# The second of two feature tiles in another order of products, and the inner operands of a Strassen-style FFN made later

## The chip, the cores and the metric

The kernel runs on one core of a Trainium2 chip. The time is the device time of one execution, in microseconds (us). The core has a matrix engine (TensorE, PE in the profile; its weight loads are listed apart as PEld), a vector engine (VectorE, DVE), a scalar engine (ScalarE, ACT), a general one (GpSimd, POOL) and a sequencer that issues DMAs (SyncE, SP). Each runs its own queue in order; they meet through semaphores. Matmuls write to accumulators in PSUM, and VectorE and ScalarE read them from there.

## The reference

One layer of a hybrid decoder for 1,048 tokens: 16 learned meta tokens and 1,024 prompt tokens as one sequence, and 8 single sample tokens with states of their own. The model width is 1,024 and the FFN width 2,816, all in float32:

```python
h = h + 0.5 * swiglu(rmsnorm(h, n1), w1g, w1u, w1d)     # first FFN
u = rmsnorm(h, nm) @ w_in                               # 4 HGRN2 heads and 8 Mamba-2 heads
...                                                     # scans, gates, norms
h = h + mix                                             # the output projection
h = h + 0.5 * swiglu(rmsnorm(h, n2), w2g, w2u, w2d)     # second FFN
y = rmsnorm(h, norm_final)
```

with `swiglu(x, wg, wu, wd) = (silu(x @ wg) * (x @ wu)) @ wd`. The change touches the gate and up half of both FFNs, `x @ wg` and `x @ wu`.

## The kernel before

**Precision.** Each float32 operand is split into a high part (a cast on ScalarE to the matmul's format) and a low part (the difference, on VectorE). A product is three matmuls, high by high, high by low, low by high (`mm3`, lines 163 to 165). Almost all matmuls of the kernel bear these three lines.

**Seven products for eight.** Gate and up projections of a feature tile of 128 columns are computed together. The weights form a 2 by 2 block matrix (gate or up, first or second half of the 1,024 rows) and the activations another (first or second half of the rows, first or second part of the tokens). Their product is made by a Winograd-Strassen scheme with seven block products, numbered 1 to 7, on sums of blocks. Tokens come in two halves c = 0, 1 of two quarters each (262 columns in the first FFN, 258 in the second). One *step* is one product on one half: four blocks of 128 rows by three matmuls, 12 matmuls. `Steps` is a list of such steps, written out by hand. `S.before(i, fn)` hangs other work ahead of step i, and `S.add(mm, post)` adds a step with what follows it. Within the two FFNs the order of PE, DVE, ACT and SP is this written order (`manual_schedule`, line 988). Outside of them a planner orders the engines other than PE by estimated times.

**Accumulators.** Products 2, 3 and 4 are added in PSUM onto 1, 5 and 7 (`Unit.bank`: `{2: 1, 3: 5, 4: 7}`); 1, 6, 5 and 7 need an accumulator of their own. `K.banks(2)` leaves two accumulators, each of two banks, one bank a token half. A new product must wait until the one that held the accumulator before has been read. Those reads are in `post` in `pair`: product 1 is copied out by ScalarE (z, line 674); product 6 is added to z (v, L676); product 2 is multiplied by the norm's factor (`times_r`, L669) and goes through SiLU (L681); product 5 is added to v (x, L683); product 7 to x (u1, L685); product 4 to v (L698), then scaled (L669) and multiplied by the gate (`product_`, L718).

**Pairs.** A loop of eleven passes, i = 0 to 10, takes two feature tiles each (`ffn`, line 993). In the passes 0 to 2 a tile has all seven products in the order 1, 6, 2, 5, 7, 3, 4, 14 steps. From i = 3 on, product 3 of the two tiles is not computed by itself: the two product-3 weight blocks and the product-3 activations form one more 2 by 2 problem, which `Inner` solves with seven smaller products. The first tile of such a pair runs 1, 6, 2, 5, 7; its product 4 comes behind the second tile's product 1 (`inner.last`). The second tile then goes on with 6, 2, 5, 7, between and behind which the inner products stand.

**Weights.** Four raw blocks a tile are loaded by SP ten or so steps ahead (`Left.load`, L452), summed on DVE (L458), cast on ACT (`hi`, L462) and given their low part on DVE (`lo`, L466). `left.plan` hangs these at steps relative to the tile's first; the last argument says at which step each product's weights are due, in the order given, and the cast is hung four steps ahead, the low part three. The inner weights have L597 and L601.

**Inner operands.** The activations of the inner problem are sums of pieces of block 3, so they are made once in an FFN. `Inner.operands` returns fourteen jobs (add back high and low part, L558; differences L571 to L574; casts L564; low parts L567) and two late ones, which `ffn` hangs at steps of the passes i = 1 and 2.

**Hidden.** The products of gate and up are stored to DRAM (`Hidden.jobs`, differences L818, stores L821 on SP) and come back for the down projection (`down`, operands split at L842 and L846, weights at L903 and L908). SP issues loads of weights and these stores in one queue.

Of the kernel before, what the change touches and what calls it, by code (L numbers as in the profile page):

```python
# [490 lines left out]
class Unit:  # L491
# [25 lines left out]
    def both(self, S):  # L517
        for p in ORDER:
            for c in range(2):
                self.step(S, p, c, (0, 1))  # L520


def halves(t):
    return t.rearrange("p (c t) -> p c t", c=2)


ORDER6 = (1, 6, 2, 5, 7, 4)


class Inner:  # L530
# [118 lines left out]
def pair(K, S, wg, wu, f, ops, spread, hid, late_r, first=None, inner=None):  # L649

    nc = K.nc
    fs = slice(f * P, f * P + P)
    s0 = len(S.steps)
    wait = late_r > 14
    tm = {}
    left = Left(K, [wg[:, 0:4, fs], wu[:, 0:4, fs], wu[:, 4:8, fs], wg[:, 4:8, fs]], 4)  # L660

    def temp(n, cs):
        if n not in tm:
            tm[n] = halves(K.t(2 * K.Q))
        return tm[n][:, cs]

    def times_r(n, i, cs, src=None):
        t = temp(n, cs)
        nc.vector.tensor_mul(t, t if src is None else src, spread.lanes(i, cs))  # L669
        return t  # L670

    def post(p, cs, b):
        if p == 1:
            nc.scalar.copy(temp("z", cs), b)
        elif p == 6:
            nc.vector.tensor_add(temp("v", cs), b, temp("z", cs))  # L676
        elif p == 2 and (f == 0 or wait and f == 1):
            nc.scalar.copy(temp("g0", cs), b)
        elif p == 2:
            t = times_r("g0", 0, cs, b)  # L680
            nc.scalar.activation(t, t, AF.Silu)  # L681
        elif p == 5:
            nc.vector.tensor_add(temp("x", cs), b, temp("v", cs))  # L683
        elif p == 7:
            nc.vector.tensor_add(temp("u1", cs), b, temp("x", cs))  # L685
            if inner:
                times_r("u1", 1, cs)
        elif p == 3:
            nc.vector.tensor_add(temp("g1", cs), b, temp("v", cs))
            if f == 0:  # L690
                return
            if wait and f == 1:
                silu(0, cs)
            silu(1, cs)
            times_r("u1", 1, cs)
        elif inner:
            t = temp("v", cs)
            nc.vector.tensor_add(t, b, t)  # L698
            tm["u0"] = tm["v"]
            times_r("u0", 0, cs)  # L700
            product_(0, cs)
        else:
            nc.vector.tensor_add(temp("u0", cs), b, temp("v", cs))
            if f == 0:
                return
            times_r("u0", 0, cs)
            for n in range(2):
                product_(n, cs)

    def silu(n, cs):  # L710
        t = times_r(f"g{n}", n, cs)
        nc.scalar.activation(t, t, AF.Silu)  # L712

    def product_(n, cs):
        if "h" not in tm:
            tm["h"] = True
            hid.append(K.slot("s", K.T))
        nc.vector.tensor_mul(halves(hid[0][:, n * 2 * K.Q : n * 2 * K.Q + 2 * K.Q])[:, cs], temp(f"g{n}", cs), temp(f"u{n}", cs))  # L718

    if inner:  # L720
        i = f % 2
        left.plan(S, s0, 0, 2 * i, ORDER6, ((0, 2, 4, 6, 8, 12), (0, 4, 6, 8, 10, 14))[i])
        unit = Unit(K, left.w, [o.op for o in ops], 4, post)

        def both(*ps):
            for p in ps:
                for c in range(2):
                    unit.step(S, p, c, (0, 1))

        def keep():  # L730
            inner.raw[i] = left.raw[3]

        cs = slice(0, 2)

        def gate():
            tm["g1"] = tm["x"]
            silu(1, cs)

        S.before(s0, keep)
        inner.then[i] = (gate, lambda: product_(1, cs))  # L740
        inner.out[i] = lambda: temp("x", cs)
        if i == 0:
            both(1, 6, 2, 5, 7)
            inner.last = lambda: both(4)
            return
        S.before(s0 + 3, lambda: inner.begin(S, s0 + 2))
        both(1)
        inner.last()
        both(6, 2, 5, 7)
        inner.step(S, 1, 6)  # L750
        inner.step(S, 5, 7)
        both(4)
        inner.step(S, 2, 3)
        inner.step(S, 4)
        e = len(S.steps)
        for at, fn in ((0, inner.then[0][0]), (2, inner.then[1][0]), (3, inner.then[0][1]), (5, inner.then[1][1])):
            S.before(e + at, fn)
        return

    if not first:  # L760
        left.plan(S, s0, int(f == 1), 3 * int(f == 1))
        Unit(K, left.w, [o.op for o in ops], 4, post).both(S)
        return

    late = {}

    def post_first(p, cs, b):

        if p == 5:
            late[p] = b  # L770
        else:
            post(p, cs, b)
            if p == 6:
                post(5, cs, late[5])

    order = first(S, left)
    unit = Unit(K, left.w, [o.op for o in ops], 4, post_first)
    for ps_ in (order[:6], order[6:]):
        for c in range(2):
            for p in ps_:  # L780
                unit.step(S, p, c, (c,), True)
    cs = slice(0, 2)
    for i, (fn, *args) in enumerate(((silu, 0, cs), (silu, 1, cs), (times_r, "u0", 0, cs), (product_, 0, cs), (times_r, "u1", 1, cs), (product_, 1, cs))):
        S.before(s0 + late_r + i, lambda fn=fn, args=args: fn(*args))
# [193 lines left out]
def ffn(K, wg, wu, wd, ops, spread, src, first, after, late_r):  # L978

    NF = DFF // P
    wgv = wg.rearrange("(k p) c -> p k c", p=P)
    wuv = wu.rearrange("(k p) c -> p k c", p=P)
    wdv = wd.rearrange("(f p) c -> p f c", p=P)
    E = mybir.EngineType

    with K.tc.manual_schedule(engines={E.PE, E.DVE, E.Activation, E.SP}):
        S = Steps()
        S.before(14, lambda: K.banks(2))  # L990
        hidden = Hidden(K)
        inner = Inner(K, ops)
        for i in range(NF // 2):
            hid, e = [], []
            rec = inner.next() if i >= 3 else None
            if i == 1:

                def operands(s0=len(S.steps) + 8):
                    made, late = inner.operands()
                    for n, fn in enumerate(made):  # L1000
                        S.before(s0 + 3 * n, fn)
                    for n, fn in enumerate(late):
                        S.before(s0 + 56 + 3 * n, fn)

                S.before(len(S.steps) + 7, operands)
            for f in (2 * i, 2 * i + 1):
                hid.append([])
                pair(K, S, wgv, wuv, f, ops, spread, hid[-1], late_r, first if f == 0 else None, rec)
                e.append(len(S.steps))
            hidden.jobs(S, i, hid, *([late_r + 6, max(late_r + 7, e[1])] if i == 0 else e), rec)  # L1010
        h = []
        down(K, S, wdv, hidden, src, h, after)
        S.run()
    return h
# [878 lines left out]
class LastFinal:  # L1893
# [11 lines left out]
    def first(self):  # L1905
        K = self.K
        self.st = K.sml.tile([P, 6, 3], F32, tag="ssl", name="ssl", bufs=1)
        self.yt = [K.slot("u", D) for i in self.tiles]
        for j, i in enumerate(self.tiles):
            ps = K.psm()  # L1910
            for k in range(4):
                self.transpose(ps, k, k, i)
            self.square(j, ps, 0, 4, 0)
            K.nc.vector.tensor_mul(self.yt[j][:, :512], ps, self.nf[0][:, :512])
# [27 lines left out]
def body(ctx, tc, a, o):  # L1942
# [86 lines left out]
    def after1(S, h, e3, e0, e1):  # L2029
# [33 lines left out]
        return nm.add  # L2063

    ffn(K, a["w_ffn1_gate"][0], a["w_ffn1_up"][0], a["w_ffn1_down"][0], ops, spread, from1, first1, after1, 26)

    constants_mix(K, a)
# [142 lines left out]
    def after3(S, h, e3, e0, e1):  # L2210
# [16 lines left out]
        return None  # L2227

    ffn(K, a["w_ffn2_gate"][0], a["w_ffn2_up"][0], a["w_ffn2_down"][0], ops2, spread2, lambda o: hd2[o], first2, after3, 14)


# [35 lines left out]
```

## Time and profile before

| | before |
|---|---|
| median of 3 runs | 1996.66 us (1996.43 to 2001.31) |
| the profiled execution | 1997.03 us, its span 1995.2 us |
| granted TensorE clock, mean | 0.992 |
| TensorE busy | 1931.3 us (97%), 16,585 matmuls |
| VectorE busy | 1532.8 us (77%) |
| ScalarE busy | 858.9 us (43%) |
| DMA | 258.45 MB, mean 130 GB/s |

The page of the profile tells for one execution how long each engine was busy, which chain of work ended last, and groups of instructions by line. Behind it stand answers of the trace: who waited for whom, busy time by stretch, and the instructions of an engine in order of time. In a timeline a row is start, length, engine, line, operation, output and inputs; in brackets is the idle time of the engine ahead of the row and what ended it. Matmuls overlap, so for TensorE the distance of two starts tells more than their lengths.

### The profile page before, as it was taken

The page shows a single profiled execution, that of the slowest core. Times are in us where ns is not written, and L with a number is a line of the kernel's source. Part 1 is how long each engine was busy: PE and PEld are TensorE (multiplying, and loading weights), DVE is VectorE, ACT ScalarE, POOL GpSimd, SP SyncE. Part 2 cuts the span into 40 slices and gives each one's busy share as a digit, 9 for nine tenths or more (in the row PEclk, how much of TensorE's full clock was granted, in tenths as well). Part 3 has the DMA queues.
Part 4 walks back from the last instruction along what each step waited for, and adds up shares of the span by engine and source line. Part 5 has one row for each costly group of instructions (what it writes and reads, how often), then busy time and mean ns, then how long its engine had stood idle before and what let it go on. Part 6 is the DMA issues. An engine that isn't in the chain of part 4 may idle for free.

```text
span 1995.2 us, 40967 instructions
## 1 busy us (share of the span) xinstructions
PE 1931.3 (97%) x16585; PEld 1889.7 (95%) x16585; DVE 1532.8 (77%) x2720; ACT 858.9 (43%) x1647; POOL 83.1 (4%) x135
## 2 busy tenths in 40 slices
PE   7999999999999999999999999999999999999997
PEld 6999999999999999998988989999999999999997
DVE  7787888888788876576755547888888888878974
ACT  7532233233533644465644535743222332354352
POOL 4000000000000410000000001200000000000000
PEclk9999999999999999999999999999999999999999
DMA  7223333335977542232532253224232333577851
GB/s 217 75 87 106 91 100 100 101 93 158 279 233 244 165 145 55 59 101 64 164 90 71 62 167 126 83 80 128 81 106 88 100 101 105 157 235 242 275 175 72
DMA packets 323877, 258.45 MB, mean 130 GB/s; under 512 B 17568, under 2 KB 299424, under 8 KB 323680
## 3 DMA queue, kind: packets, MB, share of 16 engines
q1 hardware_dynamic: 323448, 255.79, 41.9%
q8 instruction: 131, 2.15, 0.5%
q14 instruction: 58, 0.48, 0.1%
q0 software_dynamic: 224, 0.04, 0.0%
q10 hardware_dynamic: 16, 0.00, 0.0%
HBM read 190.79 MB, written 65.05 MB: 128 GB/s over the span
## 4 chain that ended last, share of the span: by engine, by line
PE 79%; DVE 12%; DMA 4%; ACT 2%; issue 2%; SPq 0%; POOL 0%; DVEq 0%; ACTq 0%; POOLq 0%
PE acc L163 23%; PE acc L165 23%; PE acc L164 23%; PE mis L163 1%; PE mis L165 1%; PE mis L164 1%; DMA r<-in_w_ffn_down_dram 1%; DVE u L352 1%; DVE s L932 1%; DVE ws L466 1%; DVE u L846 1%; DMA r<-in_w_ffn_up_dram 1%; DMA s<-in_x_prompt_dram 1%; DVE ws L908 1%; DVE t L698 1%
## 5 line engine op out<-in xcount | busy, mean ns | idle before, releaser
L163 PE MATMUL acc<-u,ws 128*128 128x258 f32 (+3 forms) x4248 | 1246.7, 294 | 23.3 <-DVE t L698 14.1
L164 PE MATMUL acc<-u,ws 128*128 128x258 f32 (+3 forms) x4248 | 1234.6, 291 | 3.1 <-DVE u L352 2.5
L165 PE MATMUL acc<-u,ws 128*128 128x258 f32 (+3 forms) x4248 | 1233.6, 291 | 3.5 <-DVE ws L466 3.4
L163 PEld LDWEIGHTS acc<-u,ws 128*128 128x128 f32 x4248 | 806.3, 190 | 32.3 <-issue 15.1
L164 PEld LDWEIGHTS acc<-u,ws 128*128 128x128 f32 x4248 | 808.8, 190 | 6.0 <-DVE u L352 3.7
L165 PEld LDWEIGHTS acc<-u,ws 128*128 128x128 f32 x4248 | 805.8, 190 | 5.0 <-DVE ws L466 4.6
L466 DVE TENSOR_TENSOR ws<-r,ws 128x512 fp32r<-128x512 f32 x276 | 190.8, 692 | 56.8 <-ACT ws L462 56.7
L462 ACT CAST ws<-r 128x512 fp32r<-128x512 f32 x276 | 158.8, 616 | 13.6 <-ACT ws L462 8.4
L681 ACT ACTIVATE t<-t 128x516 f32<-128x516 f32 (+1 forms) x41 | 26.2, 640 | 243.0 <-DVE t L669 243.0
L458 DVE TENSOR_TENSOR r<-r,r 128x512 f32<-128x512 f32 x176 | 121.0, 690 | 6.1 <-DMA r<-in_w_ffn_up_dram 4.5
L712 ACT ACTIVATE t<-t 128x524 f32<-128x524 f32 (+1 forms) x47 | 29.9, 639 | 205.7 <-DVE t L669 205.7
L846 DVE TENSOR_TENSOR u<-u,u 128x1048 fp32r<-128x1048 f32 (+3 forms) x84 | 97.0, 1157 | 5.3 <-ACT u L842 5.3
L669 DVE TENSOR_TENSOR t<-t,u 128x524 f32<-128x524 f32 (+1 forms) x135 | 92.9, 697 | 2.8
L230 POOL TENSOR_TENSOR t<-t,t 128x262 f32<-128x262 f32 (+1 forms) x56 | 54.9, 990 | 836.8 <-ACT t L229 833.6
L158 DVE TENSOR_TENSOR ws<-r,ws 128x512 fp32r<-128x512 f32 x88 | 60.0, 692 | 35.8 <-ACT ws L157 35.4
L903 ACT CAST ws<-u 128x512 fp32r<-128x512 f32 (+1 forms) x72 | 42.2, 586 | 103.1 <-DVE u L898 100.0
L842 ACT CAST u<-u 128x1048 fp32r<-128x1048 f32 (+3 forms) x84 | 82.8, 988 | 0.0
L932 DVE SCALAR_TENSOR_TENSOR s<-acc,s 128x524 f32<-128x524 f32 (+3 forms) x88 | 54.6, 643 | 36.5 <-PE acc L165 36.2
L908 DVE TENSOR_TENSOR ws<-r,ws 128x512 fp32r<-128x512 f32 (+1 forms) x84 | 57.6, 694 | 23.2 <-ACT ws L903 23.0
L903 ACT CAST ws<-r 128x512 fp32r<-128x512 f32 (+1 forms) x84 | 47.8, 581 | 62.2 <-DVE r L898 33.8
L157 ACT CAST ws<-r 128x512 fp32r<-128x512 f32 x88 | 53.5, 617 | 33.5 <-PE acc L165 29.2
L908 DVE TENSOR_TENSOR ws<-u,ws 128x512 fp32r<-128x512 f32 (+1 forms) x72 | 47.4, 659 | 26.5 <-ACT ws L903 26.5
(417 smaller groups left out, 2298.5 us busy)
## 6 DMA issues: line engine op xcount, KB each, us to landing
r<-in_w_ffn_down_dram SPq DMA_DIRECT2D x128, 256.0 KB
hd<-s SPq DMA_DIRECT2D x93, 258.0 KB
r<-in_w_ffn_gate_dram SPq DMA_DIRECT2D x88, 256.0 KB
r<-in_w_ffn_up_dram SPq DMA_DIRECT2D x88, 256.0 KB
hd<-s SPq DMA_DIRECT2D x77, 262.0 KB
u<-hd SPq DMA_DIRECT2D x36, 516.0 KB
u<-hd SPq DMA_DIRECT2D x28, 524.0 KB
r<-in_w_in_dram SPq DMA_DIRECT2D x56, 256.0 KB
```

The source lines that it names most:

```text
L163: mm(ps, whi, xhi, start=first, stop=False, skip_group_check=more)
L164: mm(ps, whi, xlo, start=False, stop=False, skip_group_check=more)
L165: mm(ps, wlo, xhi, start=False, stop=last, skip_group_check=more)
L458: self.K.nc.vector.tensor_tensor(self.raw[p], self.raw[x], self.raw[y], op)
L462: self.K.nc.scalar.copy(self.w[p][:, : self.n * P], self.raw[p])
L466: self.K.nc.vector.tensor_sub(t[:, 512 : 512 + w], self.raw[p], t[:, :w].bitcast(F32))
L669: nc.vector.tensor_mul(t, t if src is None else src, spread.lanes(i, cs))
L842: K.nc.scalar.copy(hi, lo.bitcast(F32))
L846: K.nc.vector.tensor_sub(lo, lo.bitcast(F32), hi.bitcast(F32))
L903: nc.scalar.copy(w[p, j, g][:, : n * P], src)
L908: nc.vector.tensor_sub(t[:, 512 : 512 + n * P], box[0], t[:, : n * P].bitcast(F32))
L932: nc.vector.scalar_tensor_tensor(t, b, 0.5, t, ALU.mult, ALU.add)
```

## The change

The second tile of a pair with an inner problem takes its products in the order 1, then the first tile's 4 (as before), then 2, 6, 5, 7. Before, 6 stood ahead of 2. The list of due steps, (0, 4, 6, 8, 10, 14), is the same, so the casts and low parts of the weights of 2 and 6 trade places as well. `ORDER6` becomes a pair of orders, one for each tile. The fourteen jobs of the inner operands are hung from step 18 of pass i = 1 on, 2.5 steps apart, where they were hung from step 8 on, 3 steps apart; the two late ones stay where they were (18 + 46 = 8 + 56). The loop is the same for both FFNs, so both get both parts.

```diff
-ORDER6 = (1, 6, 2, 5, 7, 4)
+ORDER6 = (1, 6, 2, 5, 7, 4), (1, 2, 6, 5, 7, 4)
...
-        left.plan(S, s0, 0, 2 * i, ORDER6, ((0, 2, 4, 6, 8, 12), (0, 4, 6, 8, 10, 14))[i])
+        left.plan(S, s0, 0, 2 * i, ORDER6[i], ((0, 2, 4, 6, 8, 12), (0, 4, 6, 8, 10, 14))[i])
...
         both(1)
         inner.last()
-        both(6, 2, 5, 7)
+        both(2, 6, 5, 7)
         inner.step(S, 1, 6)
         inner.step(S, 5, 7)
         both(4)
...
-                def operands(s0=len(S.steps) + 8):
+                def operands(s0=len(S.steps) + 18):
                     made, late = inner.operands()
                     for n, fn in enumerate(made):
-                        S.before(s0 + 3 * n, fn)
+                        S.before(s0 + 5 * n // 2, fn)
                     for n, fn in enumerate(late):
-                        S.before(s0 + 56 + 3 * n, fn)
-
-                S.before(len(S.steps) + 7, operands)
+                        S.before(s0 + 46 + 3 * n, fn)
+
+                S.before(len(S.steps) + 17, operands)
```

## The prediction

> **What bounds the kernel now.** I read the page first, then the waits of TensorE, then the busy time by stage, then the timelines of single engines around the gaps.
>
> ```profile
> span 1995.2 us, 40967 instructions
> ...
> PE 1931.3 (97%) x16585; PEld 1889.7 (95%) x16585; DVE 1532.8 (77%) x2720; ACT 858.9 (43%) x1647; POOL 83.1 (4%) x135
> ```
>
> TensorE is busy for 97% of the span, and no other engine comes near. So only two things count: where TensorE still stands, and whether the change makes it stand elsewhere. Its waits (who waited for whom: us in total, times, longest):
>
> ```profile
> PE acc L163 <- DVE t L698: 14.1, 16, 0.9
> ...
> PE mis L163 <- DVE t L643: 1.3, 2, 0.7
> ```
>
> The first row is the largest of that list by far, with 16 equal members: L698 adds product 4 of a feature tile to v, and there are eight pairs with an inner product in each of the two FFNs. Busy time by stage, for the eight pairs of the first FFN and of the second:
>
> ```profile
> 165.40:496.20 330.80, 323.08 (x2635) 321.44 (x2634) 280.03 (x475) 104.07 (x191) 0.00 (x0) 1.00 0.35 107
> 1424.00:1750.00 326.00, 318.30 (x2634) 316.23 (x2633) 278.01 (x475) 103.60 (x191) 0.00 (x0) 1.00 0.35 107
> ```
>
> The columns are length, PE, weight loads, DVE, ACT, POOL, granted clock, DMA share, GB/s. The clock is full (1.00), DMA a third used, VectorE at 85%. Weight loads leave 9.4 and 9.8 us open: all that any reordering can win there, 19.1 us. One of the 16 waits, on TensorE:
>
> ```profile
> 392.36 0.28 PE L164 MATMUL acc<-u,ws 128*128 128x262 f32 x1
> 392.49 0.28 PE L165 MATMUL acc<-u,ws 128*128 128x262 f32 x1
> 393.65 0.37 PE L163 MATMUL acc<-u,ws 128*128 128x262 f32 x1 [0.89 <-DVE t L698]
> ```
>
> Matmuls start 0.12 us apart (392.36 to 392.49), so a step of 12 takes 1.46 us. Here the next starts 1.16 us later: 1.04 us lost. (The bracket says 0.89 because a matmul's modelled end lies 0.16 us past the next one's start; add 0.15 to 0.16 to a bracket for the true loss.) What happens: there are two accumulators of two banks. The second tile's product 1 holds one until product 2 has been added. The other holds the first tile's product 7 until product 4 has been added and L698 has read it. Product 6 needs a new accumulator right behind product 4, so TensorE waits out L698.
>
> **Part 1, the second tile in the order 1, (4), 2, 6, 5, 7.** Nothing is added or removed. The same 12 matmuls, the same cast and low part, the same reads of PSUM trade two places, and the weights' casts trade places with them, so each weight stays four steps ahead. No DMA is issued elsewhere.
>
> Gain: behind product 4 now comes product 2, which needs no accumulator. It runs 2 x 1.46 = 2.9 us, and L698 (0.70) ends inside it. Product 6 then finds its accumulator free. I take the whole loss back, 16 x 1.04 = 16.6 us. Bounds: nothing, if the wait moves to another product, and the 19.1 us above. [...] The trace's 0.12 is used.
>
> What is late next? Product 5 needs the accumulator of product 2, with product 6 (2.9 us) between; product 7 needs that of product 6, with product 5 between. Before, 5 and 7 had the same distance to the reads that freed theirs, and no row shows a wait. Product 2 must also wait until ScalarE has copied product 1 out (L674); product 4 lies between.
>
> The tight place is ScalarE's queue. Now product 2's SiLU (L681) stands before the casts of product 7's weights and of the inner weights (L597); in the old order those ran ahead of it:
>
> ```profile
> 390.40 1.66 ACT L462 CAST ws<-r 128x512 fp32r<-128x512 f32 x3
> 391.96 0.62 ACT L597 CAST ws<-r 128x512 fp32r<-128x512 f32 x1
> 400.54 0.64 ACT L681 ACTIVATE t<-t 128x524 f32<-128x524 f32 x1 [7.96 <-DVE t L669]
> ```
>
> ```profile
> 392.80 0.70 DVE L698 TENSOR_TENSOR t<-acc,t 128x524 f32<-128x524 f32 x1 [1.05 <-PE acc L165]
> ...
> 396.87 0.70 DVE L676 TENSOR_TENSOR t<-acc,t 128x524 f32<-128x524 f32 x1 [0.15 <-PE acc L165]
> ...
> 399.81 0.70 DVE L669 TENSOR_TENSOR t<-acc,u 128x524 f32<-128x524 f32 x1 [1.64 <-PE acc L165]
> ```
>
> New times: product 2's multiply takes the place of product 6's add, 396.9. SiLU starts 0.73 later as it does now (399.81 to 400.54): 397.6. The cast of weight 7 follows to about 398.8 and its low part on VectorE to 399.4. Product 6's add, queued behind that low part, ends at 400.1. TensorE, now unbroken from 392.61, reaches product 7 six steps later, at 401.4: 1.3 us to spare. So cost nothing, covered by those 1.3 us; each us beyond them would cost 16 us.
>
> The end of each FFN's pairs: the last inner product already waits for L643 (1.3 us over two), because VectorE is also splitting the first operands of the down projection, which come by DMA. If those loads don't come forward with TensorE, each wait grows by up to 1.04. They are queued behind a store that waits for the product after L698, which doesn't move. Between 0 and 2.1 us; I take 0.7, nearer to 0, since casts, not landings, stand just ahead of it.
>
> **Part 2, the inner operands later.** Eleven VectorE jobs and three casts move from steps 36 to 75 of an FFN to steps 46 to 78, counted from its first step. The last cast and low part stay at steps 92 and 95. None of them is a DMA, and none is on SP or POOL. Their first reader is the first inner product, at step 106: lateness there costs nothing, as 28 steps lie between. What they leave are four small gaps (the jobs are in both FFNs):
>
> ```profile
> 97.99 0.36 PE L163 MATMUL acc<-u,ws 128*128 128x262 f32 x1 [0.28 <-DVE t L685]
> ...
> 117.77 0.36 PE L163 MATMUL acc<-u,ws 128*128 128x262 f32 x1 [2.01 <-DVE t L683]
> ...
> 139.03 0.36 PE L163 MATMUL acc<-u,ws 128*128 128x262 f32 x1 [0.38 <-ACT s L564]
> ...
> 1397.99 0.36 PE L163 MATMUL acc<-u,ws 128*128 128x258 f32 x1 [0.35 <-ACT s L564]
> ```
>
> By start to start they cost 0.43, 2.17, 0.54 and 0.51, together 3.65 us. The largest comes about so, on VectorE and on the DMA queue:
>
> ```profile
> 95.33 0.70 DVE L558 TENSOR_TENSOR u<-u,u 128x524 f32<-128x524 f32 x1
> ...
> 98.98 0.69 DVE L558 TENSOR_TENSOR u<-u,u 128x524 f32<-128x524 f32 x1
> ...
> 105.56 0.70 DVE L571 TENSOR_TENSOR u<-u 128x524 f32<-128x524 f32 x1
> 106.17 0.68 DVE L466 TENSOR_TENSOR ws<-r,ws 128x512 fp32r<-128x512 f32 x1
> 106.77 0.70 DVE L818 TENSOR_TENSOR s<-s 128x524 f32<-128x524 f32 x1
> ...
> 115.60 1.42 DVE L458 TENSOR_TENSOR r<-r,r 128x512 f32<-128x512 f32 x2 [3.02 <-DMA r<-in_w_ffn_up_dram]
> 116.93 0.69 DVE L683 TENSOR_TENSOR t<-acc,t 128x524 f32<-128x524 f32 x1
> ```
>
> ```profile
> 105.05 2.96 SPq L821 DMA_DIRECT2D hd<-s  x2
> 108.10 0.56 SPq L452 DMA_DIRECT2D r<-in_w_ffn_gate_dram  x1
> ```
>
> The weights for the next tile are issued from 108.10 on, behind a store that waits for L818. VectorE then sits 3.02 us for them and reads product 5 late. Three operand jobs (L558 twice, L571) stand ahead of L818 in a full queue, 0.61 us apart each. Gone from there, L818, the store, the loads and L683 come 3 x 0.61 = 1.83 earlier. That takes the 0.43 and 1.4 of the 2.17. At 139.03 one operand subtraction (0.61) stands just before L683 and moves behind it: I take 0.4 of 0.54, and 0.4 of 0.51 in the second FFN, since the weights' landing may bind next. Sum 2.6 us. Ends: 3.65, and a loss: at steps 56 and 58 two jobs now stand where one stood, ahead of another store and load; 0.61 late in each FFN makes -1.2 us.
>
> **Sum.** 16.6 - 0.7 + 2.6 = 18.5 us. The profiled execution took 1997.03 us (span 1995.2 and 1.8 around it), so 1978.5; it stands 0.37 above the median of the runs shown, 1996.66, which gives 1978.2.
>
> **Rivals.**
> (a) The wait moves with the shortage. Two accumulators stay two, and product 5 or 7 could pay instead. Against it: every other handover in the tile has a product between and no wait. Then only part 2 counts: about 1994, within the 0.3% (6.0 us) that a measurement here can tell from no change. [...]
> (b) Slower: ScalarE's turned order. If product 6's add ends not 1.3 us before product 7 but 1.7 us after it, TensorE waits 1.7 in each of 16 tiles, 27 us against 18.5: about 2005. It decides from (18.5 + 6)/16 = 1.5 us after, that is from 2.8 us later than reckoned, four to five VectorE jobs. For it: VectorE is at 85%, in order. Against it: the 1.64 us idle just before 399.81.
> (c) Part 2 gives nothing or its -1.2, the tail its whole 2.1: 16.6 - 2.1 - 1.2 = 13.3, about 1983.
> (d) Outside the hand-ordered FFNs a planner orders all engines but TensorE by estimated times, and its order can shift. TensorE idles 14 us there (501.15 of 515.00):
>
> ```profile
> 770.00:1285.00 515.00, 501.15 (x5008) 477.39 (x5007) 324.84 (x726) 273.92 (x559) 20.21 (x34) 0.98 0.33 99
> ```
>
> Half as much again is 7 us: about 1985 to 1990.
>
> **How the numbers follow.** The forecast 0.55, (c) 0.17, (d) 0.10, (a) 0.10, (b) 0.08. Faster by over 0.3% (under 1990.7) are the forecast, (c) and (d): 0.82; same 0.10; slower 0.08. The range runs from 1973.5 (16.6 + 3.65, no loss at the tail, and 3 us of luck in (d)'s stage) to 1989, which takes in (c) and most of (d).
>
> **What would show it.** Right: the row of L163 waiting for L698 is gone, weight loads fill all but 1 to 2 us of the eight pairs, each pair is 1.04 us shorter, the gap before product 3 near 117 us falls under 1 us, and L458's idle time for the up weights shrinks. Wrong: a row with 16 members and L669 or L676 as releaser (a), waits for L466's or L676's results at product 7 (b), or a longer stretch between the FFNs (d).

## The result and the profile after

The changed kernel takes 1976.53 us (median of 4 runs, 1973.32 to 1978.54), the kernel before 1996.8 us (median of 4, 1996.43 to 2001.31). The ratio is 0.9892, with a 95% interval from 0.9871 to 0.9913. Forecast were 1978.2 us and a range from 1973.5 to 1989. The profiled execution took 1973.32 us with a span of 1971.5; before it was 1997.03 with 1995.2, so 23.7 us less from trace to trace. The runs of both kernels spread by 5 us, and the last section shows what goes with this spread.

The page of the changed kernel, span and busy time, then the shares of the chain that ended last, then three groups (busy us, mean ns | idle time of the engine ahead of them, and what ended most of it):

```profile
span 1971.5 us, 40943 instructions
...
PE 1923.6 (98%) x16585; PEld 1885.4 (96%) x16585; DVE 1529.7 (78%) x2720; ACT 859.9 (44%) x1647; POOL 82.7 (4%) x135
...
PE 87%; DVE 7%; ACT 2%; DMA 2%; issue 1%; POOL 0%; SPq 0%; DVEq 0%; ACTq 0%; POOLq 0%
...
L163 PE MATMUL acc<-u,ws 128*128 128x258 f32 (+3 forms) x4248 | 1242.9, 293 | 6.7 <-ACT t L674 1.7
...
L466 DVE TENSOR_TENSOR ws<-r,ws 128x512 fp32r<-128x512 f32 x276 | 190.6, 691 | 75.0 <-ACT ws L462 74.9
...
L458 DVE TENSOR_TENSOR r<-r,r 128x512 f32<-128x512 f32 x176 | 121.5, 692 | 2.7 <-DMA r<-in_w_ffn_up_dram 1.2
```

The chain's shares and the same three groups on the page of the kernel before:

```profile
PE 79%; DVE 12%; DMA 4%; ACT 2%; issue 2%; SPq 0%; POOL 0%; DVEq 0%; ACTq 0%; POOLq 0%
...
L163 PE MATMUL acc<-u,ws 128*128 128x258 f32 (+3 forms) x4248 | 1246.7, 294 | 23.3 <-DVE t L698 14.1
...
L466 DVE TENSOR_TENSOR ws<-r,ws 128x512 fp32r<-128x512 f32 x276 | 190.8, 692 | 56.8 <-ACT ws L462 56.7
...
L458 DVE TENSOR_TENSOR r<-r,r 128x512 f32<-128x512 f32 x176 | 121.0, 690 | 6.1 <-DMA r<-in_w_ffn_up_dram 4.5
```

Read them together. The chain that ended last runs through TensorE for 87% of the span where it was 79%, and less through VectorE and DMA. TensorE's idle time ahead of L163 falls by 16.6 us, and L698 is no longer named there. (That 16.6 is also the forecast of part 1 is chance: these idle times are sums of brackets, and the four small gaps are among them.) VectorE's idle time ahead of the weights' low parts (L466) rises by 18.2 us: the waiting did not vanish, it moved to an engine that can afford it. VectorE's idle time for the up weights (L458) falls from 4.5 to 1.2 us.

Busy time of the eight pairs, in the columns that the prediction explains (the windows are shortened, the second is moved; they start at other steps than those before, and the second holds 24 matmuls more):

```profile
165.40:487.00 321.60, 321.00 (x2634) 320.79 (x2633) 278.50 (x475) 102.98 (x189) 0.00 (x0) 1.00 0.36 110
1413.00:1733.00 320.00, 319.33 (x2658) 318.68 (x2658) 279.14 (x480) 103.09 (x190) 0.00 (x0) 1.00 0.36 110
```

Weight loads now leave 0.8 and 1.3 us open, where they left 9.4 and 9.8. Windows that hold the same work as those before, 161.50 to 483.20 and 1409.70 to 1726.80, leave 0.8 and 1.3 as well. So this stage has next to nothing left for a reordering to win.

The span splits at the reads of product 4 (L698: count, shortest, median and longest in ns, first and last start), here for the two FFNs before:

```profile
L698 DVE TENSOR_TENSOR t<-acc,t x16: 693/700/704, 186.0 to 498.4; 128x524 f32<-128x524 f32 x16
L698 DVE TENSOR_TENSOR t<-acc,t x16: 685/693/696, 1444.3 to 1752.3; 128x516 f32<-128x516 f32 x16
```

and after:

```profile
L698 DVE TENSOR_TENSOR t<-acc,t x16: 693/700/704, 182.1 to 485.4; 128x524 f32<-128x524 f32 x16
L698 DVE TENSOR_TENSOR t<-acc,t x16: 684/692/697, 1430.0 to 1729.1; 128x516 f32<-128x516 f32 x16
```

Differences of these starts give five stretches of the span (us; the experiments follow below, and in some of them, not in this table, the read has another line number):

| kernel | to the first read | 16 reads, first FFN | between | 16 reads, second FFN | to the end |
|---|---|---|---|---|---|
| before | 186.0 | 312.4 | 945.9 | 308.0 | 242.9 |
| changed | 182.1 | 303.3 | 944.6 | 299.1 | 242.4 |
| order only | 184.9 | 303.3 | 944.6 | 299.1 | 242.4 |
| operands only | 183.5 | 312.4 | 945.0 | 308.1 | 242.3 |
| changed, again | 182.2 | 303.3 | 947.7 | 299.2 | 242.5 |

From the first to the last read an FFN holds its eight waits, and these stretches shrink by 9.1 and 8.9 us, 18.0 in all: that is the new order. The stretch ahead of the first read loses 3.9 us. A wait of TensorE ahead of all that the change touches stands at 86.00 us before and at 85.39 after, so 0.6 of this is not the change's; the 3.3 left hold three of the four small gaps of part 2. The fourth is in the 1.3 us of the middle stretch. The last 0.5 us was not looked into. In its second profile the changed kernel takes 947.7 us for the middle stretch, so a difference of 1.3 us there says little by itself.

### The profile page after: what moved, and what is told of

It reads as the page before. It is cut to its first block, busy times and chain, and to the rows that moved or that the text cites. A ratio compares the mean times of both kernels' runs of the same rounds, so it can differ in the third digit from the quotient of the medians.

```text
span 1971.5 us, 40943 instructions
## 1 busy us (share of the span) xinstructions
PE 1923.6 (98%) x16585; PEld 1885.4 (96%) x16585; DVE 1529.7 (78%) x2720; ACT 859.9 (44%) x1647; POOL 82.7 (4%) x135
## 4 chain that ended last, share of the span: by engine, by line
PE 87%; DVE 7%; ACT 2%; DMA 2%; issue 1%; POOL 0%; SPq 0%; DVEq 0%; ACTq 0%; POOLq 0%
PE acc L163 26%; PE acc L165 26%; PE acc L164 26%; PE mis L163 1%; PE mis L165 1%; PE mis L164 1%; DVE u L352 1%; DMA s<-in_x_prompt_dram 1%; PE mis L1725 1%; PE mis L1449 0%; PE mis L1782 0%; DVE ws L466 0%; PE mis L1445 0%; DVE u L341 0%; DVE t L301 0%
## 5 line engine op out<-in xcount | busy, mean ns | idle before, releaser
L163 PE MATMUL acc<-u,ws 128*128 128x258 f32 (+3 forms) x4248 | 1242.9, 293 | 6.7 <-ACT t L674 1.7
L163 PEld LDWEIGHTS acc<-u,ws 128*128 128x128 f32 x4248 | 803.9, 189 | 12.2 <-ACT t L674 2.1
L466 DVE TENSOR_TENSOR ws<-r,ws 128x512 fp32r<-128x512 f32 x276 | 190.6, 691 | 75.0 <-ACT ws L462 74.9
L458 DVE TENSOR_TENSOR r<-r,r 128x512 f32<-128x512 f32 x176 | 121.5, 692 | 2.7 <-DMA r<-in_w_ffn_up_dram 1.2
L846 DVE TENSOR_TENSOR u<-u,u 128x1048 fp32r<-128x1048 f32 (+3 forms) x84 | 97.0, 1156 | 5.3 <-ACT u L842 4.5
L669 DVE TENSOR_TENSOR t<-t,u 128x524 f32<-128x524 f32 (+1 forms) x135 | 92.9, 697 | 2.8
```

The costliest lines, as they stand in the source:

```text
L163: mm(ps, whi, xhi, start=first, stop=False, skip_group_check=more)
L458: self.K.nc.vector.tensor_tensor(self.raw[p], self.raw[x], self.raw[y], op)
L466: self.K.nc.vector.tensor_sub(t[:, 512 : 512 + w], self.raw[p], t[:, :w].bitcast(F32))
L846: K.nc.vector.tensor_sub(lo, lo.bitcast(F32), hi.bitcast(F32))
```

## The experiments

Two theories were tried against others. By the first (handover), the 16 waits are product 6 waiting for the accumulator that product 4's read frees, and an accumulation put between covers them. By the second (queue), the small gaps come from operand jobs that stand ahead of a store's subtraction (L818) and of the reads in VectorE's queue. The main rival is the shortage of accumulators, by which a wait comes back at another product.

**The new order alone.** The operand jobs go back to their old steps:

```diff
-                def operands(s0=len(S.steps) + 18):
+                def operands(s0=len(S.steps) + 8):
...
-                        S.before(s0 + 5 * n // 2, fn)
+                        S.before(s0 + 3 * n, fn)
...
```

> Part 1 alone: the new order, the inner operands at their old steps. Handover theory (each of the 16 waits is the read of product 4's accumulator by L698 plus a restart; 1.37 us from the last matmul before the gap at 392.49 to the second after it at 393.86, less two spacings of 0.12, is 1.13 us each): the 16 waits are gone, a pair takes 40.22 us instead of 41.36 in the first FFN and 39.66 instead of 40.77 in the second, 18.0 us together; the four gaps of part 2 stay; about 1978.8 us. Rival (the parts need each other, or half of the gain is drift outside the FFNs): pairs shorter than 41.36 by less than 0.8 us, or another line takes the wait; 1984 us or more.

Measured: 1979.35 us (1976.12 to 1984.4, 4 runs), ratio 0.9908 (0.9887 to 0.9929) against 2000.18 us (7 runs) of the kernel before on that chip. In the table its 16 reads take exactly as long as the changed kernel's, 303.3 and 299.1, and the waits for L698 are gone. Two of the small gaps stay:

```profile
97.75 0.36 PE L163 MATMUL acc<-u,ws 128*128 128x262 f32 x1 [0.29 <-DVE t L685]
...
117.19 0.36 PE L163 MATMUL acc<-u,ws 128*128 128x262 f32 x1 [1.66 <-DVE t L683]
```

The two near 139 and 1398 us are absent here, although the jobs stand where they stood. VectorE's wait for the up weights shortly ahead of 139 us, in the kernel before and here:

```profile
136.24 1.42 DVE L458 TENSOR_TENSOR r<-r,r 128x512 f32<-128x512 f32 x2 [0.77 <-DMA r<-in_w_ffn_up_dram]
```

```profile
135.09 1.42 DVE L458 TENSOR_TENSOR r<-r,r 128x512 f32<-128x512 f32 x2 [0.22 <-DMA r<-in_w_ffn_up_dram]
```

It is 0.55 us shorter here, as much as the gap there was. In the second FFN the wait of the same kind is 0.68 us in the kernel before and 0.23 here. So whether these gaps open hangs on when a load lands, as well as on the jobs.

**The operands alone.** The converse, on the kernel before:

```diff
-                def operands(s0=len(S.steps) + 8):
+                def operands(s0=len(S.steps) + 18):
...
-                        S.before(s0 + 3 * n, fn)
+                        S.before(s0 + 5 * n // 2, fn)
...
```

> Part 2 alone: the inner operands later, the old order. Queue theory (three operand jobs, 0.61 us each, stand ahead of the difference whose store holds back the weights' loads): the gaps before the matmuls that were at 97.99, 117.77, 139.03 and 1397.99 us are gone or under 0.2 us, the loads are issued 1.8 us earlier against TensorE's steps, the 16 waits for L698 stay; 3.65 us and four restarts of 0.09, so about 1992.7 us. Rival (the 117.77 gap is a late landing that the queue has little to do with): 1.5 us or more of that gap stays, about 1994.5 us.

Measured: 1991.96 us (1990.21 to 1993.25, 4 runs), ratio 0.9962 (0.9947 to 0.9977). All four gaps are gone, and the span is 3.9 us shorter than in the kernel before's profile. The large row stays:

```profile
PE acc L163 <- DVE t L698: 14.1, 16, 0.9
```

In the traces the two parts do not touch each other: 18.0 us by the one, some 4 by the other, 22 by both. The times do not show it as cleanly: on this chip the medians differ by 20.8 us for the order alone and by 8.2 for the operands alone, twice what the stretches show. The kernel before took 1995.76 to 2002.65 us there, at mean granted clocks of 0.990 to 0.992, the operands alone ran at 0.991 to 0.995; so the split is read from the traces.

**Three operand jobs alone.** Of the kernel before's jobs only the first three move behind L818, the next two to steps just behind them:

```diff
-                        S.before(s0 + 3 * n, fn)
+                        S.before(s0 + (10, 12, 15, 16, 17, 15)[n] if n < 6 else s0 + 3 * n, fn)
```

> The kernel before with only the first three operand jobs moved from steps 36, 39, 42 to 46, 48, 51 (and the two that need them to 52 and 53); the other nine stay. Queue theory: these three stood ahead of the store and the loads, so the gaps at 98 and 118 us go, the loads come 1.8 us earlier against TensorE's steps; the gap near 139 us, which came and went with the landing of the weights (0.54, 0, 0.52 us in three runs with the old steps), may be there or not; 2.6 us less. Rival (all jobs must leave the stretch, or the 118 gap is a matter of the landing alone): 1 us or more of the 118 gap stays.

Measured: 1998.6 us in its one run, a time that the mixing stage between the FFNs sets (949.7 us there, against 945.9). The stretch to the first read is 183.6 us, 2.4 shorter. The gaps at 98 and 118 us are gone, so moving these jobs is enough to end both. In the profiles that keep the old steps (the kernel before, the order alone, and the old order with a second read below) the gap near 118 is there with brackets of 2.01, 1.66 and 1.55. With the later jobs unmoved, a gap near 137 us (bracket 0.65) stays in place of that at 139, and one of 0.78 near 1399 us in place of that at 1398.

**Product 4 read twice, old order.** VectorE reads the first tile's product 4 once more ahead of L698, into a tile that nobody uses; the outputs stay the same:

```diff
             t = temp("v", cs)
+            if f % 2 == 0:
+                nc.vector.tensor_add(temp("d", cs), b, t)
             nc.vector.tensor_add(t, b, t)
```

> The kernel before, but VectorE reads the first tile's product 4 twice (the first sum is thrown away), so its accumulator comes free one operation, 0.61 to 0.73 us, later. Handover theory: each of the 16 gaps grows by as much, a pair takes 42.0 to 42.1 us in the first FFN instead of 41.36; 16 x 0.65 = 10 us longer, about 2007 us. Rival (TensorE waits there for product 6's weights or for something else that ends at the same time): gap and pair stay, 1997 us.

Measured: 2012.69 us. Two added lines make L698 L700 here. The 16 waits grow with the read:

```profile
PE acc L163 <- DVE t L700: 25.9, 16, 1.6
```

25.9 less 14.1 is 11.8, or 0.74 for each wait; the 16 reads of both FFNs take 317.5 and 313.2 us, 5.1 and 5.2 more over seven pairs. So the wait's end is this read.

**Product 4 read twice, new order.** The same edit on the changed kernel.

> The changed kernel with the same second read of product 4. Handover theory: product 2 (2.9 us) covers both reads (1.4 us), no wait for product 4's read, a pair takes 40.22 us as without it, about 1976.5 us. Shortage theory (two accumulators stay too few, the new order only just hides it): a new wait of 0.3 us or more in each of the 16 tiles, 1981 us or more.

Measured: 1986.5 us. No wait for product 4's read came back: the new order does take it off TensorE's path. But another appeared, in seven of eight pairs of each FFN:

```profile
PE acc L163 <- DVE t L669: 5.8, 14, 0.6
```

One of them on TensorE:

```profile
213.55 0.28 PE L165 MATMUL acc<-u,ws 128*128 128x262 f32 x1
214.07 0.36 PE L163 MATMUL acc<-u,ws 128*128 128x262 f32 x1 [0.24 <-DVE t L669]
```

This is product 7 of the next pair's first tile, which waits until L669 has read product 2. A read added in one tile is still felt half a pair later, because VectorE's queue does not catch up. 0.52 less 0.12 is 0.40 us lost for 0.73 added (the distance of the two reads, 182.40 to 183.13 in the first pair), so 0.33 was to spare. In the second FFN 0.75 was lost (1467.87 to 1468.74), so nothing was to spare. The prediction had named 1.3 us of room at the second tile's product 7 and had looked no further. The wait for L643 at the end of each FFN grows too, from 1.3 to 2.6 us over two. By the time and the waits, this run lies on the side of the shortage theory; whether the accumulators or VectorE's lateness set the new wait is told by the experiment on ScalarE's order below.

**Two more adds in the second tile.** L676, the add of product 6, is done three times, with the same result:

```diff
             nc.vector.tensor_add(temp("v", cs), b, temp("z", cs))
+            if inner and f % 2:
+                for _ in range(2):
+                    nc.vector.tensor_add(temp("v", cs), b, temp("z", cs))
```

> The changed kernel, with the add of the second tile's product 6 (L676) done three times over, the same result each time: two more VectorE operations, 1.2 to 1.5 us, ahead of everything behind it on VectorE. Forecast's reckoning (1.3 us to spare, at the second tile's product 7): no wait or one under 0.2 us there, pairs at 40.2 to 40.4. VectorE-chain theory (the run with two reads of product 4 shows 0.3 us to spare in the first FFN and none in the second, at the next first tile's product 7, which waits for L669): waits for L669 of 0.9 to 1.4 us in 14 of 16 pairs, pairs at 41.1 to 41.6 and 40.9 to 41.3 us, 16 to 20 us more in all.

Measured: 2004.38 us. The row that appears is that of the last experiment, not one of product 7 in the second tile:

```profile
PE acc L163 <- DVE t L669: 8.7, 14, 0.6
```

At the second tile's product 7 itself the list shows nothing, but the starts do. VectorE's three adds (the second and third are L679) and TensorE there, in the first FFN:

```profile
397.09 0.70 DVE L676 TENSOR_TENSOR t<-acc,t 128x524 f32<-128x524 f32 x1
397.82 1.44 DVE L679 TENSOR_TENSOR t<-acc,t 128x524 f32<-128x524 f32 x2
```

```profile
399.20 0.28 PE L165 MATMUL acc<-u,ws 128*128 128x262 f32 x1
399.41 0.36 PE L163 MATMUL acc<-u,ws 128*128 128x262 f32 x1
```

The adds end at 399.26 instead of 397.79, 1.47 us later, and product 7 starts 0.21 - 0.12 = 0.09 us late. So the room there was 1.38 us; in the second FFN it was 1.26 (0.20 lost for 1.46). Forecast were 1.3. The binding place is the other one again, the next first tile's product 7, with 0.78 us lost in seven of eight pairs, less than the 0.9 to 1.4 expected; in the second FFN that tile's product 5 waits 0.32 us as well, for L676.

**Whose order used up the room.** The kernel with the second read of product 4, and the cast of product 7's weights hung one step earlier, ahead of product 2's SiLU in ScalarE's queue:

```diff
-        left.plan(S, s0, 0, 2 * i, ORDER6[i], ((0, 2, 4, 6, 8, 12), (0, 4, 6, 8, 10, 14))[i])
+        left.plan(S, s0, 0, 2 * i, ORDER6[i], ((0, 2, 4, 6, 8, 12), (0, 4, 6, 8, 9, 14))[i])
```

> The changed kernel with product 4 read twice, which cost a wait for L669 in 14 pairs (pairs of 40.70 and 40.37 us), and now the cast of the second tile's weights of product 7 hung one step earlier, so that ScalarE does it ahead of product 2's SiLU as in the old order. Turned-order theory (VectorE stands 1.22 us for that cast, which the old order had ready; that wait uses up the room): VectorE's wait there shrinks by 0.6 us or more, the waits for L669 go in the first FFN and nearly so in the second, pairs at 40.22 to 40.3 and 39.66 to 39.8. Rival (VectorE is simply full): waits stay at 0.4 and 0.75 us.

Measured: 1976.58 us, and no wait for L669 is left. The reason can be read in the changed kernel's own timelines of ScalarE and VectorE:

```profile
387.73 0.64 ACT L681 ACTIVATE t<-t 128x524 f32<-128x524 f32 x1 [5.82 <-DVE t L669]
388.28 0.60 ACT L462 CAST ws<-r 128x512 fp32r<-128x512 f32 x1
```

```profile
387.00 0.69 DVE L669 TENSOR_TENSOR t<-acc,u 128x524 f32<-128x524 f32 x1
388.92 0.69 DVE L466 TENSOR_TENSOR ws<-r,ws 128x512 fp32r<-128x512 f32 x1 [1.22 <-ACT ws L462]
389.53 0.70 DVE L676 TENSOR_TENSOR t<-acc,t 128x524 f32<-128x524 f32 x1
```

ScalarE idles 5.82 us for SiLU's input, and the cast behind it could have run in that time. VectorE then idles 1.22 us for the cast. With the cast ahead of SiLU, the group's idle time falls back below that of the kernel before:

```profile
L466 DVE TENSOR_TENSOR ws<-r,ws 128x512 fp32r<-128x512 f32 x276 | 191.2, 694 | 55.4 <-ACT ws L462 55.3
```

75.0 less 55.4 is 19.6 us, or 1.22 for each of 16 tiles. So VectorE's lost room came from ScalarE's order, and the wait for L669 went with the same two accumulators.

**The same order in the first tile.** Products 2 and 6 trade places in the first tile of a pair too, where no product 4 stands between 1 and 2:

```diff
-ORDER6 = (1, 6, 2, 5, 7, 4), (1, 2, 6, 5, 7, 4)
+ORDER6 = (1, 2, 6, 5, 7, 4), (1, 2, 6, 5, 7, 4)
...
-            both(1, 6, 2, 5, 7)
+            both(1, 2, 6, 5, 7)
```

> The changed kernel with the order 1, 2, 6, 5, 7 in the first tile as well, where no other product lies between 1 and 2. Handover theory: what took the wait away in the second tile is the product that lies between a product and the read it needs, so here product 2 waits for ScalarE's copy of product 1 (L674, 0.60 us, where the waits for L698 with 0.70 us cost 1.13): a gap of about 1.1 us start to start in each of the 16 first tiles, a pair takes 41.2 us in the first FFN, 16 us more in all, about 1993 us. Rival (product 2 ahead of 6 is the better order by itself): no new wait, pairs stay at 40.22 and 39.66.

Measured: 2004.87 us. The row that takes the place of L698's:

```profile
PE acc L163 <- ACT t L674: 20.6, 18, 1.3
```

Product 2 adds onto product 1's accumulator, and ScalarE must have copied product 1 out (L674). One such place on TensorE:

```profile
206.94 0.28 PE L165 MATMUL acc<-u,ws 128*128 128x262 f32 x1
208.41 0.39 PE L163 MATMUL acc<-u,ws 128*128 128x262 f32 x1 [1.19 <-ACT t L674]
```

1.35 us are lost there, more than at the old place. The 16 reads take 313.6 and 309.4 us, 10.3 more in each FFN where 8 were expected; most of the rest above the expected 1993 is the stage between the FFNs, 951.6 us here. In this kernel the order 1, 2, 6 by itself is a loss; it wins only where another product stands between 1 and 2.

**The tail.** The changed kernel with product 7's cast early and the first operands of the down projection split a little later:

```diff
-            at = [b + k for k in (-14, -11, -11, -9, -9, -7)], [b + k for k in (-8, -7, -6, -5, -4, -2)]
+            at = [b + k for k in (-14, -11, -11, -9, -9, -7)], [b + k for k in (-8, -7, -5, -4, -3, -2)]
```

> The changed kernel with the cast of the second tile's product-7 weights one step earlier, and at the head of the down projection the split of its third, fourth and fifth operand blocks hung one step later, so that one 1.2 us low part (L846) stands behind the inner product's L643 and no longer ahead of it. Theory: the waits for L643 at the end of both FFNs (0.77 and 0.83 us and a restart each) go, the early cast adds room on VectorE and no time: 1.7 us less than the changed kernel in the profile, too little to be told from it by the times. Rival (VectorE is full there, the wait moves to the next accumulator or to the down projection's first operands): the stretches keep their length.

Beside it the changed kernel on the same chip:

> The changed kernel itself, on the same chip as the run beside it and in more rounds. If the 23.7 us between the two profiled executions are the change, the sum of the stretches gives 22 (18.0 from the pairs, 4 from the passes 1 and 2 and the second FFN) and the rest is drift; the ratio to before should lie at 0.989, within 0.987 to 0.991.

Measured: 1977.09 us (1975.71 to 1980.12, 4 runs), ratio 0.9904 (0.9888 to 0.9921), and for the changed kernel 1978.27 us (1974.03 to 1980.76, 4 runs), ratio 0.9903 (0.9886 to 0.992). In the trace the waits for L643 are gone, and the 16 reads take 302.4 and 298.3 us, 0.9 and 0.8 less, the 1.7 us that were expected. The times cannot tell the two kernels apart. The last wait of this kind in the changed kernel:

```profile
481.60 0.28 PE L165 MATMUL mis<-u,ws 128*128 128x262 f32 x1
482.48 0.39 PE L163 MATMUL mis<-u,ws 128*128 128x262 f32 x1 [0.60 <-DVE t L643]
```

## Why the prediction was right, step by step

**Part 1, the gain.** Right in mechanism, small in size: 18.0 us against 16.6. The term that was mis-sized is the price of one wait, 1.04 us. The starts of the first tile's L698 give it, before:

```profile
392.80 0.70 DVE L698 TENSOR_TENSOR t<-acc,t 128x524 f32<-128x524 f32 x1 [1.05 <-PE acc L165]
...
434.16 0.70 DVE L698 TENSOR_TENSOR t<-acc,t 128x524 f32<-128x524 f32 x1 [1.05 <-PE acc L165]
```

and after:

```profile
383.17 0.70 DVE L698 TENSOR_TENSOR t<-acc,t 128x524 f32<-128x524 f32 x1 [1.05 <-PE acc L165]
...
423.39 0.70 DVE L698 TENSOR_TENSOR t<-acc,t 128x524 f32<-128x524 f32 x1 [1.06 <-PE acc L165]
```

A pair takes 41.36 us before and 40.22 after: 1.14 less, not 1.04. The tenth of a microsecond between them was lost behind the wait (last section).

**What is late next.** Partly wrong. The 1.3 us at the second tile's product 7 was right: the added adds measured 1.38 and 1.26. But this was not the tightest place. Product 7 of the next first tile had 0.33 us in the first FFN and nothing in the second, as the second read of product 4 shows. Nothing was lost by it, but the margin that the prediction gave was not the margin there was.

**ScalarE's turned order.** The step that SiLU would stand ahead of product 7's cast, and hold up VectorE, is in the trace (1.22 us of idle time, 16 times). That it costs nothing in the changed kernel is right, too.

**The tail, -0.7.** Wrong: 0. The waits for L643 were 0.61 and 0.67 us by their brackets before, and together 1.3 us in both kernels. The prediction had made it hang on the loads of the down projection's operands. In the first FFN these did not come forward: the store ahead of them is issued 2.21 us behind the last pair's first L698 in both kernels (475.52 to 477.73, and 463.61 to 465.82). The first split of an operand (L846) came forward all the same, from 11.73 us behind that L698 (487.25) to 10.60 (474.21). So the landings did not hold up the splits there.

**Part 2, 2.6.** Too low: 3.1 of it stood in the three gaps ahead of the pairs and 0.5 in the second FFN, and all went. The step that failed is the limit put on the gap at 117.77. L818 was reckoned to come 1.83 us earlier:

```profile
104.31 0.70 DVE L818 TENSOR_TENSOR s<-s 128x524 f32<-128x524 f32 x1
...
111.39 1.41 DVE L458 TENSOR_TENSOR r<-r,r 128x512 f32<-128x512 f32 x2
112.72 0.70 DVE L683 TENSOR_TENSOR t<-acc,t 128x524 f32<-128x524 f32 x1
```

It comes 2.46 earlier (106.77 to 104.31), and the loads are issued from 105.64 instead of 108.10, by as much. 0.6 of that is the whole kernel's earlier start. VectorE's two sums of weights, however, come 4.21 earlier (115.60 to 111.39) and no longer wait. So the landing came forward by more than the issue. The prediction had held it fixed at the issue's distance. Why the load landed faster was not settled. The loss of 1.2 us at the other end of the term did not come: after the change TensorE has no gap between 86 and 176 us, nor around 1398.

**The rivals.** (a), a wait that moves with the shortage of accumulators, is refuted for this kernel: 16 gaps of about 1.04 us are gone with the same two accumulators. (b), the slower case, did not come, though its mechanism did eat the room. (c) gave too little. (d), a longer stretch between the FFNs, did not come: it took 945.9 us before and 944.6 and 947.7 in the changed kernel's two profiles. (The upper figure of its forecast has no term behind it: 1978.2 and 7 make 1985, not 1990.)

**The sum.** 18.0 by the order and some 4 by the operands make 22 of the 23.7 us between the two traces, against 18.5 forecast. The rest is the earlier start (0.6 us), the shorter middle stretch and the 0.5 us at the end. The medians differ by 20.3 us, near to the forecast's 18.5 because the changed kernel's other runs, up to 1978.54, were slower than its profiled one. So the mechanisms were right, but all three terms were put too low, and that the median lies within 2 us of the forecast is in part luck.

## What to carry to other kernels

Where an accumulation can be put onto an accumulator that is held anyway, put it behind the product whose read frees the next accumulator: here the order alone took the read off TensorE's path, 16 waits and 18.0 us. After a wait is gone, go through every later handover of the period, into the next tile as well, since the room can be used up at another place than the one next to the edit; an added read or add on VectorE measures it (0.33 us there in the first FFN, 1.38 next to the edit). In an in-order queue, hang work that is ready ahead of an activation that still waits for TensorE: the cast hung ahead of SiLU goes with 55.4 us of idle time on VectorE ahead of L466, the cast behind it with 75.0.

## What the runs showed of the hardware

**A wait cost more than its length.** In the first FFN of the kernel before, the first matmul of 262 columns behind a wait for L698 lasts 0.36 or 0.37 us where those behind it last 0.28 or 0.29. Behind the wait that the prediction shows it starts at 393.65, and the next at 393.86:

```profile
393.86 0.28 PE L164 MATMUL acc<-u,ws 128*128 128x262 f32 x1
393.98 0.29 PE L165 MATMUL acc<-u,ws 128*128 128x262 f32 x1
```

That is 0.21 us instead of 0.12, so 0.09 is lost in addition to the 1.04. Over 16 waits this makes the 1.4 us by which 18.0 exceeds 16.6.

**In the mixing stage the granted clock halved for 3.4 us at a time, and how often differed from run to run.** Stretches of 3.40 us in the changed kernel's mixing stage, the granted clock third from the right:

```profile
926.50:929.90 3.40, 1.45 (x45) 1.09 (x44) 2.88 (x8) 1.69 (x4) 0.00 (x0) 1.00 1.01 281
929.90:933.30 3.40, 2.94 (x35) 2.91 (x36) 2.31 (x6) 1.59 (x5) 0.00 (x0) 0.50 0.64 178
933.30:936.70 3.40, 3.40 (x83) 3.16 (x83) 2.23 (x7) 1.01 (x4) 0.00 (x0) 0.99 0.58 173
```

TensorE was busy for 1.45 us of the first, and the clock is 0.50 in the second. The changed kernel's profile has four such stretches between its FFNs, that of the kernel before five, the changed kernel's second profile six, and that of the kernel with two more adds ten, in a stage that none of the edits touches. Their spans and mean clocks:

```profile
core 0: 1971.5 us, clock 0.994
```

```profile
core 0: 2002.7 us, clock 0.987
```

The stretch between the FFNs takes 944.6 and 951.1 us in these two, with VectorE busy for 679.03 and 678.78 us of it. Over the twelve profiles of this study the stretch takes 944.6 us with four of them (twice), 945.0 to 946.3 with five, 947.7 and 947.9 with six, 948.3 to 949.7 with seven, and 951.6 and 951.1 with nine and ten. So it goes with the spread of the profiles; which of the two makes the other was not tried apart. For runs without a profile only the mean clock is on record, and it does not order the changed kernel's four runs strictly (0.994, 0.992, 0.992 and 0.990 for 1973.32, 1974.84, 1978.23 and 1978.54 us). This is why the one run of the two more adds, and the single runs of other experiments, are told by their pairs here and not by their times. Why the clock was halved more often in one run than in another was not tried.
